# First norm of a one-layer trunk: conditioning by column blocks between the tiles of x, seven first units built tile by tile

## The chip, the cores and the metric

The kernel runs on one core of one Trainium2 chip. The number that counts is device time in microseconds (us) of one execution, as the median of several. The engines are named as the profile names them: PE multiplies matrices (PEld is its weight load), DVE, ACT and POOL work element by element, SP issues the transfers.

## The reference

One inference step of a trunk with one layer: 1024 latent tokens and 128 context tokens of width 1024 go through a SwiGLU block, a token mixer (attention and a gated recurrence) and a second SwiGLU block, each on a normalised and conditioned input. What matters here is the input of the first SwiGLU block:

```python
mod_p = (silu(c_ctx) @ w_ada[l] + b_ada[l]).reshape(1, N_MOD, D_MODEL)          # context
mod_s = (silu(c) @ w_ada[l] + b_ada[l]).reshape(c.shape[0], N_MOD, D_MODEL)     # latent
x = x + 0.5 * m[2] * swiglu(modulate(x, norm_g[0], m[0], m[1]), *ffn1)
def modulate(x, g, shift, scale): return rmsnorm(x, g) * (1.0 + scale) + shift
def swiglu(h, w1, w3, w2): return (silu(h @ w1) * (h @ w3)) @ w2
```

Shift is `m[0]`, scale is `m[1]`: 1024 numbers each for latent and for context, made from two vectors and 1024x2048 weights. The hidden width is 2816, that is 22 blocks of 128.

## The kernel before

**Layout.** Features lie on the partitions. `x` is eight tiles `x0`..`x7` of 128 features by 1152 tokens (latent first, then context). The tokens are cut into four quarters of 288 (`QW`), taken in the order `QS` = 3, 0, 1, 2; quarter 3 holds both kinds of tokens. A product in full precision is three matmuls on operands split into a high and a low part (`mm3`: high weight by high x, high weight by low x, low weight by high x).

**The first norm is folded.** The first block's units multiply the weights by `x * gs`, where `gs` is gain times (1 + scale). `split` makes the high part `bh` on ACT and the low part `bl` on DVE for one quarter of one tile (quarter 3 in two pieces of 160 and 128 tokens). The factor of each token, `rs`, is multiplied in when a unit is read out of PSUM, and the shift comes in as a bias, which is the shift vector through the same weights. A unit `(j, q)` is one of the two weight matrices (`j` = 0 for w1, 1 for w3) by one quarter: eight tiles of three matmuls, 24 in all, into one PSUM bank.

**`start`** is what comes first. It runs in four steps. First, all eight tiles are squared on ACT and summed on DVE (`stat_first`), and `stat_three` sums over partitions on PE (`nps`) and forms `rs` by Ln, Exp and a correction of three DVE operations. Second, `ada_pe(1, ...)` multiplies both vectors by the 1024x1024 scale weights: eight transfers of 512 KB (`wada`), each followed by four PE matmuls into four groups of 32 partitions; ACT copies the sums (`adar`), PE turns them (`adat`), DVE adds the bias (`modt`) and forms all of `gs`. Third, the first weights w1 and w3 were split in between (`hl`), and eight tiles are split and multiplied into six units (`up` and `dn` hold three banks each; `st` and `ps1` one each); `ada_pe(0, ...)`, the same for shift, is advanced between the tiles. Fourth, the shift is written as two extra columns beside quarter 3 (`shift`), and 16 small matmuls `pb` form the bias of the first block.

**After it**, `plain_block` runs four hidden blocks (`f` = 0 to 3) in this way, with the other two units of block 0 first; `after()` advances, between the units, `whole`, which forms the normalised input `hx` and writes it to memory (`hd`), and from block 2 on `sums`, which reads it back and forms the combined operands of the later blocks. The other 18 hidden blocks use those (`fast_block`).

**What sets the order.** Each engine runs its instructions in one order, and waits at an instruction until its operands are there; a scheduler fixes that order when the program is built. Instructions recorded under `pin` (`keep_in_program_order`) keep the order of the code on their engine. All transfers are issued by SP.

Of the kernel before, what the change touches and what calls it, by code (L numbers as in the profile page):

```python
# [9 lines left out]
F32 = mybir.dt.float32  # L10
# [83 lines left out]
class Trunk:  # L94
# [27 lines left out]
    def start(self):  # L122
        nc, a, pp = self.nc, self.a, self.pp
        self.sc = self.fp.tile([P, KT, 32], F32, name="sc")
        nc.vector.memset(self.sc, 0.0)
        nc.scalar.activation(self.sc[:, :, 0:2], self.cc, AF.Silu)
        pin = self.tc.keep_in_program_order
        wada = lambda k: self.wide("wada")
        raw = [self.wide("raw0")[:, :D].rearrange("p (k m) -> p k m", k=KT) for _ in range(2)]
        self.x = [self.tt(F32, f"x{k}") for k in range(KT)]  # L130
        self.new_rs()
        for k in range(KT):
            nc.sync.dma_start(self.x[k][:, :T], a["xT"][k])
            if k in (2, 4):
                nc.sync.dma_start(raw[k // 2 - 1], a["w13"][0, 0, k // 2 - 1])
        for k in range(KT):
            for c in ORDER:
                self.stat_first(c, k, pin)
        self.stat_three(pin)
        ws = [self.hl(raw[j], [P, KT, P], nc.vector, pin) for j in range(2)]  # L140
        for _ in self.ada_pe(1, wada, pin):
            pass
        self.alloc_b(0)
        units = [(0, q) for q in QS] + [(1, q) for q in QS[:2]]
        ps = {u: self.bank(("up", "dn")[i // 3], "ps") for i, u in enumerate(units)}
        m0 = self.ada_pe(0, wada, pin)
        for k in range(KT):
            for q in QS:
                self.split(q, k, pin)
            if k == KT - 1:  # L150
                w1 = self.load_w(a["w13"][0, 1, 0], KT, P, pin)
            for j, q in units:
                (wh, wl), (xh, xl) = ws[j], self.B[q][k // 4]
                term = wh[:, k], wl[:, k], xh[:, k % 4, :QW], xl[:, k % 4, :QW]
                self.mm3(ps[j, q], [term], start=k == 0, stop=k == KT - 1)
            for _ in range((0, 0, 0, 1, 2, 2, 2, 1)[k]):
                next(m0)
        next(m0, None)
        self.pre = ws, (w1, self.load_w(a["w13"][0, 1, 1], KT, P, pin))
        self.shift()  # L160
        self.early, self.bias = ps, []
        for j in range(2):
            pb = pp.tile([P, 2], F32, tag="ps1", bufs=1, name="pb")
            for k in range(KT):
                nc.tensor.matmul(pb, raw[j][:, k], self.modt[:, 0, k], start=k == 0, stop=k == KT - 1)
            bias = self.cp.tile([P, 2], F32, tag="bias", bufs=6, name="bias")
            nc.vector.tensor_copy(bias, pb)
            self.bias.append(bias)
# [86 lines left out]
    def ada_pe(self, m, buf, pin=lambda i: i):  # L255
        nc, a = self.nc, self.a
        ps = self.pp.tile([P, 256], F32, tag="ps1", bufs=1, name="adap")
        for k in range(KT):
            w = buf(k)[:, :D]
            pin(nc.sync.dma_start(w, a["w_ada"][k * P : (k + 1) * P, m * D : (m + 1) * D]))  # L260
            for g in range(4):
                pin(
                    nc.tensor.matmul(
                        ps[32 * g : 32 * g + 32, :],
                        self.sc[:, k, :],
# [166 lines left out]
    def stat_first(self, c, k, pin):  # L432
# [5 lines left out]
        if k:  # L438
            pin(nc.vector.tensor_add(acc, acc, sq))
# [1846 lines left out]
```

## Time and profile before

| | |
|---|---|
| runs | 2874.91, 2879.49, 2879.66 us; median 2879.49 |
| span of the profiled execution | 2874.3 us |
| busy share of the span | PE 97%, PEld 92%, DVE 70%, ACT 46%, POOL 34% |
| transfers | 331.76 MB, mean 115 GB/s |
| PE before its first matmul | 20.17 us |
| first matmul of hidden block 0 | 34.48 us |
| first matmul of hidden block 1 | 74.31 us |

The page gives no time of the profiled execution beside its span; what lies around the span is taken as the difference to the median, 5.2 us. Times of rows count from the start of the span. In a row of the timeline the columns are the start, the length, the engine, the line of the code, the operation, what it writes and reads with its shape, and how many instructions the row holds; a bracket gives idle time ahead of it and what ended that. In a row of groups the columns behind the count are the busy time, the mean length in ns, and the idle time ahead. In a row of windows they are the stretch, its length, the busy time of PE, PEld, DVE, ACT and POOL with their counts, the granted clock of PE (1.00 is full), the share of transfer engines in use and GB/s.

### The profile page before, as it was taken

Reading aid. Unit: us, or ns where it says so; the run is one execution under the profiler, and the core shown is the slowest. Engines: PE = TensorE matmul, PEld = TensorE weight load, DVE = VectorE, ACT = ScalarE, POOL = GpSimd, SP = SyncE. Lnnn points to the kernel's source line nnn. Section 1 sums busy time; section 2 is a strip of 40 time slices with the busy share of each in tenths; the row PEclk is TensorE's granted clock in tenths of the full one; section 3 lists DMA queues with packets and bytes.
Section 4 is the critical chain, followed back from the end, with each engine's and each line's share of the span. In section 5 each row is a group of like instructions: output and inputs, shape, how many; then the busy total and the mean of one; then the engine's idle time right before and its main releaser. Section 6 shows DMA issues by size and latency. Waiting matters only on the chain. (4 is left out here: it accounts for less than half of the span.)

```text
span 2874.3 us, 55665 instructions
## 1 busy us (share of the span) xinstructions
PE 2778.7 (97%) x21138; PEld 2641.1 (92%) x21138; DVE 2025.9 (70%) x4425; ACT 1331.1 (46%) x2738; POOL 966.0 (34%) x1005
## 2 busy tenths in 40 slices
PE   6999999999999999999999999989999999999998
PEld 5999999999989999988998787779989999999997
DVE  7677777577778877877355777756675666568875
ACT  6432322322166677767535777730552222236332
POOL 0133233354222122222144444532452443334450
PEclk9999999999999999999999999999999999999999
DMA  6643333663121111112412001262553443447631
GB/s 237 211 142 128 125 125 117 216 209 116 61 84 55 50 57 37 57 44 71 165 60 79 18 14 31 71 221 82 177 173 100 154 146 122 138 139 213 205 100 67
DMA packets 218940, 331.76 MB, mean 115 GB/s; under 512 B 24048, under 2 KB 142768, under 8 KB 218672
## 3 DMA queue, kind: packets, MB, share of 16 engines
q1 hardware_dynamic: 218672, 328.20, 35.0%
q8 instruction: 167, 2.74, 0.4%
q14 instruction: 101, 0.83, 0.1%
HBM read 244.93 MB, written 83.18 MB: 114 GB/s over the span
## 5 line engine op out<-in xcount | busy, mean ns | idle before, releaser
L1746 PE MATMUL b<-xo,wo 128*128 128x288 f32 x3552 | 482.3, 295 | 0.3 <-DVE et L1752 0.3
L1746 PEld LDWEIGHTS b<-xo,wo 128*128 128x128 f32 x3552 | 474.3, 188 | 0.6 <-DVE et L1752 0.6
L1746 PE MATMUL b<-bh,wo 128*128 128x288 f32 x1776 | 365.0, 295 | 2.1 <-ACT et L1756 2.1
L473 PE MATMUL mm<-xh,wh 128*128 128x384 f32 (+1 forms) x1008 | 352.1, 349 | 10.9 <-DVE sg L750 5.6
L474 PE MATMUL mm<-xl,wh 128*128 128x384 f32 (+1 forms) x1008 | 341.9, 339 | 0.0
L475 PE MATMUL mm<-xh,wl 128*128 128x384 f32 (+1 forms) x1008 | 341.3, 339 | 0.0
L1746 PEld LDWEIGHTS b<-bh,wo 128*128 128x128 f32 x1776 | 288.6, 188 | 2.3 <-ACT et L1756 2.3
L502 DVE SCALAR_TENSOR_TENSOR x<-dn,modt,x 128x256 f32<-128x256 f32 (+4 forms) x472 | 225.6, 499 | 89.5 <-PE dn L475 88.4
L1746 PE MATMUL b<-bl,wo 128*128 128x288 f32 x888 | 261.4, 294 | 0.0
L473 PEld LDWEIGHTS mm<-xh,wh 128*128 128x128 f32 (+1 forms) x1008 | 189.4, 188 | 20.8 <-DVE sg L750 7.4
L1720 ACT CAST wo<-raw 128x512 fp32r<-128x512 f32 x185 | 114.7, 621 | 183.9 <-issue 78.9
L474 PEld LDWEIGHTS mm<-xl,wh 128*128 128x128 f32 (+1 forms) x1008 | 189.4, 188 | 2.3 <-issue 0.7
L475 PEld LDWEIGHTS mm<-xh,wl 128*128 128x128 f32 (+1 forms) x1008 | 189.1, 188 | 1.0
L1946 PE MATMUL d<-xd,wd 128*128 128x288 f32 x1344 | 181.4, 297 | 6.6 <-DVE x L1933 5.9
L1946 PEld LDWEIGHTS d<-xd,wd 128*128 128x128 f32 x1344 | 179.9, 190 | 8.0 <-DVE x L1933 2.8
L318 DVE SCALAR_TENSOR_TENSOR junk<-wada,cb 128x512 bf16<-128x512 f32 x224 | 164.4, 734 | 14.1 <-DMA wada<-in_w_aT 13.3
L1721 DVE TENSOR_TENSOR wo<-raw,wo 128x512 fp32r<-128x512 f32 x185 | 127.4, 689 | 65.3 <-ACT wo L1720 62.6
L1461 POOL TENSOR_TENSOR ehl<-e,ehl 128x512 fp32r<-128x512 f32 x93 | 122.1, 1317 | 141.6 <-ACT ehl L1459 76.2
L1746 PEld LDWEIGHTS b<-bl,wo 128*128 128x128 f32 x888 | 167.1, 188 | 0.0
L247 POOL TENSOR_TENSOR wl<-raw,wh 128x1024 fp32r<-128x1024 f32 (+3 forms) x51 | 101.2, 1985 | 171.1 <-ACT wh L246 154.8
L1720 ACT CAST wo<-ws 128x512 fp32r<-128x512 f32 x74 | 45.6, 618 | 225.9 <-POOL ws L1716 216.9
L1721 DVE TENSOR_TENSOR wo<-ws,wo 128x512 fp32r<-128x512 f32 x74 | 71.6, 968 | 109.3 <-ACT wo L1720 109.0
(441 smaller groups left out, 7193.4 us busy)
## 6 DMA issues: line engine op xcount, KB each, us to landing
raw<-in_w SPq DMA_DIRECT2D x148, 256.0 KB, 3.5
wada<-in_w_aT SPq DMA_DIRECT2D x112, 256.0 KB, 3.1
raw<-in_w SPq DMA_DIRECT2D x42, 512.0 KB, 3.8
raw<-in_w_in SPq DMA_DIRECT2D x41, 512.0 KB, 3.5
xr<-xd SPq DMA_DIRECT2D x56, 288.0 KB, 3.7
hr<-hs SPq DMA_DIRECT2D x26, 576.0 KB, 5.7
hb<-hd SPq DMA_DIRECT2D x44, 288.0 KB, 3.4
hs<-et SPq DMA_DIRECT2D x84, 144.0 KB, 2.1
```

Source lines behind the costliest of these rows:

```text
L247: pin((eng or self.nc.gpsimd).tensor_sub(wl, raw, wh))
L318: nc.vector.scalar_tensor_tensor(junk, ws[n % 2], 1.0, cs[s], ALU.mult, ALU.mult, accum_out=o)
L473: pin(nc.tensor.matmul(ps, wh, xh, start=start and i == 0, stop=False))
L474: pin(nc.tensor.matmul(ps, wh, xl, start=False, stop=False))
L475: pin(nc.tensor.matmul(ps, wl, xh, start=False, stop=stop and i == n - 1))
L502: nc.vector.scalar_tensor_tensor(self.x[m][:, a:b], ps[:, a - lo : b - lo], self.modt[:, gm, m, s : s + 1], self.x[m][:, a:b], ALU.mult, A ...
L1461: eng.tensor_sub(el, e, eh)
L1720: nc.scalar.copy(wh, src[i])
L1721: nc.vector.tensor_sub(wl, src[i], wh)
L1746: nc.tensor.matmul(ps, w[:, k], x[:, k, :QW], start=first, stop=last, skip_group_check=home != i)
L1946: nc.tensor.matmul(ps, w[:, k], xv, start=start, stop=stop, skip_group_check=home != i)
```

## The change

The conditioning weights for scale and shift are laid out by blocks of 128 output columns (`w_a01`), one block for each tile of `x`. The transfers now go tile by tile: w1, tile 0, its two blocks of conditioning weights (512 KB each), w3, tile 1, its two blocks, and so on, all pinned. For each tile, `sums` multiplies both vectors by the two blocks in 16 PE matmuls, ACT copies the result, and `vectors` turns it by one matmul with a selector that also adds the two halves; four small DVE operations make `gs` and the shift of that tile, and the shift's high and low part as two extra columns of quarter 3. `split` of tile k then runs quarter by quarter, each followed by its units; seven of the eight units of block 0 grow tile by tile. The `sums` of tile k + 1 stand behind the units of quarter 3 of tile k, its `vectors` behind those of quarter 0. The squares of tile k + 1 (two halves of 576 tokens) follow the splits of tile k on ACT and are added on POOL, those of the last tile on DVE. Behind the last tile `stat` and `root` form `rs` in three chunks between the quarters, the eighth unit (w3 by quarter 2) runs as a whole, and `pb` is gone: the two extra columns of the units (0, 3) and (1, 3) are the bias. `whole` is advanced in block 1 only.

The new `start`, and the other places, cut to their core (the old `start`, `ada_pe`, `shift`, `stat_first` and `stat_three` are removed):

```diff
     def start(self):
+        nc, a, pp, fp = self.nc, self.a, self.pp, self.fp
         pin = self.tc.keep_in_program_order
+        sc = fp.tile([P, KT, 32], F32, name="sc")
+        nc.vector.memset(sc, 0.0)
+        nc.scalar.activation(sc[:, :, 0:2], self.cc, AF.Silu)
+        sel = fp.tile([P, 2, 2], F32, name="sel")
+        iv = self.ident.rearrange("p (v h r) -> p v h r", v=2, h=2)
+        nc.vector.tensor_add(sel, iv[:, :, 0, 0:2], iv[:, :, 1, 0:2])
+        b1 = fp.tile([P, KT], F32, name="b1")
+        nc.vector.tensor_scalar(b1, self.bada[:, 1], 1.0, None, ALU.add)
+        raw = [self.wp.tile([P, KT, P], F32, tag="raw", bufs=2, name="raw") for _ in range(2)]
         self.x = [self.tt(F32, f"x{k}") for k in range(KT)]
         self.new_rs()
+        self.alloc_b(0)
+        wa = {}
+
+        def load(what):
+            for c in what:
+                if c in "ab":
+                    j = "ab".index(c)
+                    pin(nc.sync.dma_start(raw[j], a["w13"][0, 0, j]))
+                elif c == "w":
+                    k = len(wa)
+                    wa[k] = [self.wide("wada")[:, :D].rearrange("p (k n) -> p k n", k=KT) for _ in range(2)]
+                    for v in range(2):
+                        pin(nc.sync.dma_start(wa[k][v], a["w_a01"][k, v]))
+                else:
+                    k = int(c)
+                    pin(nc.sync.dma_start(self.x[k][:, :T], a["xT"][k]))
+
+        def sums(k):
+            ps = pp.tile([P, P], F32, tag="ps1", bufs=1, name="adap")
+            for i in range(4):
+                for g in range(4):
+                    n = 4 * (g % 2) + i
+                    pin(
+                        nc.tensor.matmul(
+                            ps[32 * g : 32 * g + 32, :],
+                            sc[:, n, :],
+                            wa[k][g // 2][:, n, :],
+                            start=(i == 0),
+                            stop=(i == 3),
+                            tile_position=(0, 32 * g),
+                            skip_group_check=True,
+                        )
+                    )
+            row = fp.tile([P, P], F32, tag="hf", bufs=self.hfb, name="adar")
+            pin(nc.scalar.copy(row, ps))
+            return row
+
+        def vectors(k, row):
+            ps = pp.tile([P, 2, 2], F32, tag="ps1", bufs=1, name="adat")
+            pin(nc.tensor.matmul(ps, row, sel, start=True, stop=True))
+            ng = self.ng[:, 0, k : k + 1].to_broadcast([P, 2])
+            pin(nc.vector.scalar_tensor_tensor(self.gs[:, 0, k], ps[:, 1], b1[:, k : k + 1], ng, ALU.add, ALU.mult))
+            sh = self.modt[:, 0, k]
+            pin(nc.vector.tensor_scalar(sh, ps[:, 0], self.bada[:, 0, k : k + 1], None, ALU.add))
+            hi, lo = [t[:, k % 4, QW : QW + 2] for t in self.B[QS[0]][k // 4]]
+            pin(nc.vector.tensor_copy(hi, sh))
+            pin(nc.vector.tensor_sub(lo, sh, hi))
+
+        def square(k):
+            for v in range(2):
+                c = ts(v, 2 * QW)
+                sq = self.rs[:, c] if k == 0 else self.half("sq")
+                pin(nc.scalar.activation(sq, self.x[k][:, c], AF.Square))
+                if k:
+                    pin((nc.vector if k == KT - 1 else nc.gpsimd).tensor_add(self.rs[:, c], self.rs[:, c], sq))
+
+        load("a0wb1w")
+        ws = [self.hl(raw[j], [P, KT, P], nc.vector, pin) for j in range(2)]
+        square(0)
+        vectors(0, sums(0))
+        rest = iter(("2w", "3w", "4w", "5w", "6w", "7w", "", ""))
+        homes = {(0, 3): "up", (1, 3): "dn", (0, 0): "up", (1, 0): "dn", (0, 1): "up", (1, 1): "dn", (0, 2): "st"}
+        cols = {q: QW + 2 * (q == QS[0]) for q in QS}
+        ps = {u: self.bank(t, "ps", cols[u[1]]) for u, t in homes.items()}
+
+        def unit(j, q, k):
+            (wh, wl), (xh, xl), n = ws[j], self.B[q][k // 4], cols[q]
+            term = wh[:, k], wl[:, k], xh[:, k % 4, :n], xl[:, k % 4, :n]
+            self.mm3(ps[j, q], [term], start=k == 0, stop=k == KT - 1, pin=pin)
+
+        var = []
+
+        def stat(c):
+            p = pp.tile([P, CW], F32, tag="ps1", bufs=1, name="nps")
+            cs = slice(c * CW, (c + 1) * CW)
+            pin(nc.tensor.matmul(p, self.ones, self.rs[:, cs], start=True, stop=True))
+            v = self.half("var")[:, :CW]
+            pin(nc.scalar.copy(v, p))
+            var.append((self.rs[:, cs], v))
+
+        def root():
+            r, v = var.pop(0)
+            t = fp.tile([P, CW], F32, tag="hf", bufs=self.hfb, name="rt")
+            pin(nc.scalar.activation(r, v, AF.Ln, bias=self.epst))
+            pin(nc.scalar.activation(r, r, AF.Exp, scale=-0.5))
+            pin(nc.vector.scalar_tensor_tensor(t, v, EPS, r, ALU.add, ALU.mult))
+            pin(nc.vector.scalar_tensor_tensor(t, t, -0.5, r, ALU.mult, ALU.mult))
+            pin(nc.vector.scalar_tensor_tensor(r, t, 1.5, r, ALU.add, ALU.mult))
+
         for k in range(KT):
+            load(next(rest))
+            last = k == KT - 1
+            if last:
+                self.lnexp()
+            for i, q in enumerate(QS):
+                self.split(q, k, pin)
+                unit(0, q, k)
+                if q != QS[-1]:
+                    unit(1, q, k)
+                if last:
+                    if i:
+                        root()
+                    if i < 3:
+                        stat(ORDER[i])
+                elif i == 0:
+                    row = sums(k + 1)
+                elif i == 1:
+                    vectors(k + 1, row)
+            if not last:
+                square(k + 1)
+        w1 = self.load_w(a["w13"][0, 1, 0], KT, P, pin)
+        ps[1, QS[-1]] = self.bank("ps1", "ps")
         for k in range(KT):
+            unit(1, QS[-1], k)
         self.pre = ws, (w1, self.load_w(a["w13"][0, 1, 1], KT, P, pin))
+        self.early = ps
...
         early = not l and not f
         for j, q in order:
             wh, wl = ws[j]
-            if early and (j, q) in self.early:
+            n = QW + (2 if not l and q == QS[0] else 0)
+            if early:
                 ps = self.early[j, q]
             else:
-                n = QW + (2 if not l and f and q == QS[0] else 0)
                 ps = self.bank("up", "ps", n)
...
-            if early:
-                bias[j] = self.bias[j]
+            if n > QW:
+                bias[j] = self.cp.tile([P, 2], F32, tag="bias", bufs=6, name="bias")
+                nc.vector.tensor_copy(bias[j], ps[:, QW:n])
...
                 if l and f == 0:
                     next(self.tail, None)
-                elif f < 2 - l:
+                elif f == 1 - l:
                     next(steps, None)
-                else:
+                elif f:
                     next(sums, None)
...
-    a["w_ada"] = f("w_ada")[0]
+    a["w_a01"] = f("w_ada")[0][:, : 2 * D].reshape(KT, P, 2, KT, P).transpose(3, 2, 1, 0, 4)
```

The order on PE at the start before: all three sums over partitions (`nps`), then all 32 matmuls of the scale (`adap`), two turns (`adat`), and only then the first unit (`ps`, with `bh`, `bl` the split of x and `wh`, `wl` that of the weight).

```order
L446 MATMUL nps<-rs,ones 128x384 x3
L263 MATMUL adap<-wada,sc 32x256 x32
L278 MATMUL adat<-ident,adar 128x128 x2
L473 MATMUL ps<-bh,wh 128x288
L474 MATMUL ps<-bl,wh 128x288
L475 MATMUL ps<-bh,wl 128x288
```

The order on PE now, in the middle of tile 1 (the end of the sums for tile 2, `adap_271`; the two units of quarter 0, `ps_184` and `ps_185`; the turn for tile 2, `adat_298`; the first unit of quarter 1, `ps_186`):

```order
L159 MATMUL adap_271<-wada_190,sc_100 32x128 x2
L159 MATMUL adap_271<-wada_191,sc_100 32x128 x2
L497 MATMUL ps_184<-bh_118,wh_147 128x288
L498 MATMUL ps_184<-bl_119,wh_147 128x288
L499 MATMUL ps_184<-bh_118,wl_148 128x288
L497 MATMUL ps_185<-bh_118,wh_151 128x288
L498 MATMUL ps_185<-bl_119,wh_151 128x288
L499 MATMUL ps_185<-bh_118,wl_152 128x288
L175 MATMUL adat_298<-sel_103,adar_288 128x4
L497 MATMUL ps_186<-bh_122,wh_147 128x288
```

The conditioning of the next tile now stands inside the units of each tile.

DVE before, from the one `gs` of all tiles on: nothing stands between the low parts of one tile and those of the next.

```order
L334 SCALAR_TENSOR_TENSOR gs_93<-modt_92,vec_68 128x16
L467 SCALAR_TENSOR_TENSOR bl_292<-x0_105,gs_93,bh_291 128x160
L467 SCALAR_TENSOR_TENSOR bl_292<-x0_105,gs_93,bh_291 128x128
L467 SCALAR_TENSOR_TENSOR bl_280<-x0_105,gs_93,bh_279 128x288
L467 SCALAR_TENSOR_TENSOR bl_284<-x0_105,gs_93,bh_283 128x288
L467 SCALAR_TENSOR_TENSOR bl_288<-x0_105,gs_93,bh_287 128x288
L467 SCALAR_TENSOR_TENSOR bl_292<-x1_106,gs_93,bh_291 128x160
```

DVE now, in tile 0 (`bl_119`, `bl_123`, `bl_127` are the low parts of quarters 0, 1 and 2; `gs_93`, `modt_92` and the two small ones behind them belong to tile 1):

```order
L491 SCALAR_TENSOR_TENSOR bl_119<-x0_109,gs_93,bh_118 128x288
L177 SCALAR_TENSOR_TENSOR gs_93<-adat_231,b1_105,vec_68 128x2
L179 TENSOR_SCALAR modt_92<-adat_231,vec_68 128x2
L181 CAST bh_130<-modt_92 128x2
L182 TENSOR_TENSOR bl_131<-modt_92,bh_130 128x2
L491 SCALAR_TENSOR_TENSOR bl_123<-x0_109,gs_93,bh_122 128x288
L491 SCALAR_TENSOR_TENSOR bl_127<-x0_109,gs_93,bh_126 128x288
L491 SCALAR_TENSOR_TENSOR bl_131<-x1_110,gs_93,bh_130 128x160
```

The low part of quarter 1 now stands behind the four small operations for the next tile.

POOL now, from its first work on; before, the six `wl` (L247) came first and nothing stood ahead of them.

```order
L2297 UNCONDITIONAL_BRANCH
L190 ISA
L190 TENSOR_TENSOR rs<-rs,sq 128x576 x12
L330 TENSOR_TENSOR wl<-raw,wh 128x1024 x6
L1740 TENSOR_TENSOR ws<-raw 128x256 x2
```

Twelve additions of squares moved from DVE to POOL.

DVE now, at the last tile (`rt` and `rs` are the root of one chunk, `sl` a unit's read-out):

```order
L491 SCALAR_TENSOR_TENSOR bl_121<-x7_116,gs_93,bh_120 128x288
L221 SCALAR_TENSOR_TENSOR rt_676<-var_666,rs_117 128x384
L222 SCALAR_TENSOR_TENSOR rt_676<-rt_676,rs_117 128x384
L223 SCALAR_TENSOR_TENSOR rs_117<-rt_676,rs_117 128x384
L1692 TENSOR_TENSOR sl_755<-ps_182,rs_117 128x288
L491 SCALAR_TENSOR_TENSOR bl_125<-x7_116,gs_93,bh_124 128x288
L221 SCALAR_TENSOR_TENSOR rt_694<-var_684,rs_117 128x384
L222 SCALAR_TENSOR_TENSOR rt_694<-rt_694,rs_117 128x384
L223 SCALAR_TENSOR_TENSOR rs_117<-rt_694,rs_117 128x384
L1692 TENSOR_TENSOR sl_759<-ps_184,rs_117 128x288
L491 SCALAR_TENSOR_TENSOR bl_129<-x7_116,gs_93,bh_128 128x288
```

The low parts of the last two quarters stand behind the roots of the first two chunks.

100 lines of the change are left out of this document (3 added, 97 removed).

## The prediction

> **What bounds the kernel now.** I read the page first, then PE by stretches, then PE's order of time up to hidden block 1, then the prices of single operations.
>
> ```profile
> span 2874.3 us, 55665 instructions
> PE 2778.7 (97%) x21138; PEld 2641.1 (92%) x21138; DVE 2025.9 (70%) x4425; ACT 1331.1 (46%) x2738; POOL 966.0 (34%) x1005
> ...
> 20.00:40.00 20.00, 14.94 (x101) 9.16 (x102) 14.00 (x32) 13.49 (x28) 0.00 (x0) 0.83 0.84 325
> 60.00:74.30 14.30, 14.03 (x90) 13.44 (x83) 11.14 (x33) 13.24 (x19) 2.36 (x1) 0.76 0.34 106
> 74.40:99.60 25.20, 25.20 (x192) 25.20 (x191) 10.74 (x30) 10.67 (x21) 4.79 (x2) 1.00 0.82 272
> 99.60:124.90 25.30, 25.30 (x192) 25.30 (x192) 24.80 (x59) 12.47 (x29) 5.06 (x2) 1.00 0.63 200
> 124.90:150.10 25.20, 25.20 (x192) 25.20 (x191) 15.64 (x32) 10.05 (x20) 4.66 (x5) 1.00 0.50 148
> ```
>
> PE is the bound, and from hidden block 1 on it has no gap: 25.20 of 25.20 us for 192 matmuls. So whatever moves the start of block 1 moves the end by as much, and the change is judged by that one moment.
>
> ```profile
> PE nps L446 <- DVE rs L439: 20.2, 1, 20.2
> 31.08 1.01 PE L263 MATMUL adap<-wada,sc 128*32 128x256 f32 x8 [1.63 <-DMA wada<-in_w_ada]
> 34.48 0.61 PE L473 MATMUL ps<-bh,wh 128*128 128x288 f32 x1 [1.23 <-ACT bh L466]
> 62.17 1.95 PE L165 MATMUL pb<-modt,raw 128*128 128x2 f32 x16 [0.27 <-DVE modt L279]
> 65.39 3.48 PE L165 MATMUL pb<-modt,raw 128*128 128x2 f32 x16
> 74.31 0.29 PE L473 MATMUL ps<-bh,wh 128*128 128x290 f32 x1
> ```
>
> PE waits 20.2 us for the squares and then for the scale weights; units run from 34.48 with no wait worth naming, `pb` takes 5.4 us, and block 1 starts at 74.31. The change works on these 74.31 us.
>
> **Its parts, and the sum.** Removed: `pb` (5.4 us of PE, and 0.76 of the clock around it), the wait for all squares and all scale weights. The eight units of block 0 stay: 192 matmuls. The transfers are the same bytes in another order; their pace:
>
> ```profile
> GB/s 0 76 238 326 412 426 418 424 408 430 399 412 414 410 407 407 393 139 382 404 418 421 410 407 262 11 0 0 0 0 0 52 246 393 311 333 74 79 270 0
> 11.99 2.78 ACT L437 ACTIVATE sq<-x 128x384 f32<-128x384 f32 x6 [1.37 <-DMA x<-in_xT]
> ```
>
> Slices are 1.5 us: 1.58 MB are in at 7.5 us, then 0.41 MB each us. The fourth tile (3.0 MB in that order) is there by this count at 11.0, and ACT got it at 11.99: 1 us from bytes to use. Now w1, tile 0, two blocks and w3 are 2.8 MB with the constants: 10.5 + 1.1 = 11.6 us. ACT splits w3 only then (1.0), squares tile 0 (two of 576: 1.25) and copies the sums; with the turn and `gs` (1.2) the first split starts at 15.1; its two pieces (0.8) and six matmuls at half clock (1.5) bring PE to the sums of tile 1 at 17.4. A tile and its blocks are 1.64 MB, 4.0 us. If transfers set the pace, tile 7 would be there near 40 us.
>
> They don't, as the order shows: a tile is one chain across PE, ACT and DVE. Its prices:
>
> ```profile
> 49.02 1.07 PE L263 MATMUL adap<-wada,sc 128*32 128x256 f32 x16
> 50.02 0.40 PE L473 MATMUL ps<-bh,wh 128*128 128x288 f32 x1
> ...
> 50.39 0.30 PE L475 MATMUL ps<-bh,wl 128*128 128x288 f32 x1
> 50.52 0.30 PE L473 MATMUL ps<-bh,wh 128*128 128x288 f32 x1
> 60.49 0.37 ACT L275 COPY adar<-adap 128x256 f32<-128x256 f32 x1 [7.39 <-PE adap L263]
> 60.99 0.38 PE L278 MATMUL adat<-ident,adar 128*128 128x128 f32 x2
> L466 ACT ACTIVATE bh<-x,gs 128x288 fp32r<-128x288 f32 x24 | 11.0, 525 | 0.0
> L467 DVE SCALAR_TENSOR_TENSOR bl<-x,gs,bh 128x288 fp32r<-128x288 f32 x24 | 11.0, 514 | 0.1
> 33.50 0.17 DVE L334 SCALAR_TENSOR_TENSOR gs<-modt,vec 128x16 f32<-128x16 f32 x1
> ```
>
> From the sums of tile k + 1 to those of tile k + 2: 16 matmuls over the same columns as the eight at 49.02, 1.00; copy 0.37; high part of quarter 0, 0.52; its low part, 0.51; the five matmuls that wait for it, 0.135 each, 0.67; the turn, between half of 0.38 and all of it, 0.25; `gs`, shift and its two parts, three lengths of 0.17, 0.5; low part of quarter 1, 0.51; then 5 + 3 + 6 matmuls, 1.89; six hand-overs, 0.5 (the first matmul after a switch lasts 0.40 against 0.30; as much is taken for the others). Sum 6.7 us, and nothing of it overlaps, since each engine keeps its order. ACT's other work (two more quarters, two squares) fits beside it.
>
> The additions on POOL are the next term. Before, POOL had nothing to do here. What it does to DVE is seen later:
>
> ```profile
> 98.74 0.45 DVE L1633 TENSOR_TENSOR xo<-hd,xo 128x288 fp32r<-128x288 f32 x1
> 101.07 2.46 POOL L247 TENSOR_TENSOR wl<-raw,wh 128x1024 fp32r<-128x1024 f32 x1 [10.36 <-ACT wh L246]
> 101.19 2.65 DVE L1633 TENSOR_TENSOR xo<-hd,xo 128x288 fp32r<-128x288 f32 x1
> 145.44 1.95 POOL L1716 TENSOR_TENSOR ws<-raw 128x256 f32<-128x256 f32 x2 [27.00 <-DVE bl L1594]
> 146.72 0.98 DVE L1683 SCALAR_TENSOR_TENSOR sl<-hf,bias,sl 128x288 f32<-128x288 f32 x1
> 151.97 0.51 DVE L1683 SCALAR_TENSOR_TENSOR sl<-hf,bias,sl 128x288 f32<-128x288 f32 x1
> L2089 POOL TENSOR_TENSOR hl<-hr,hh 128x576 fp32r<-128x576 f32 x4 | 6.0, 1516 | 1.9 <-PE d L1946 1.9
> ```
>
> A DVE operation of 0.45 that starts behind a POOL operation lasts 2.65 us, to just behind POOL's end; one of the form of `bl`, with two operands in SBUF, goes from 0.51 to 0.98. So DVE stands still for the length of the POOL operation. An addition of 576 is 1.38 in proportion to 1024 in 2.46, and 1.52 in the row of 576 with its waits; I take 1.42. There are two for each of tiles 1 to 6. The first is ready when half the tile is squared, on ACT 2.3 us behind the sums (copy 0.37, three quarters at 11.0 / 24, half a square 0.6); `gs` comes 2.6 us behind them (0.37 + 0.52 + 0.51 + 0.67 + 0.25 and hand-overs). So they take the port first: the cast of the shift waits for the first, its low part for the second, and the low part of quarter 1 starts at 6.2 instead of 4.2. I take +2.1 a tile, cycle 8.8 (ends: 0, and 2 x 1.52 = 3.0).
>
> That leaves PE all but idle for about 3.1 us in each tile. What gaps do to its clock:
>
> ```profile
> 168.00:171.00 3.00, 2.04 (x16) 1.81 (x14) 0.58 (x1) 0.62 (x1) 3.00 (x5) 1.00 0.05 19
> 171.00:174.00 3.00, 1.84 (x13) 1.85 (x14) 2.96 (x8) 2.26 (x5) 0.10 (x1) 1.00 0.09 18
> ...
> 1527.40:1529.40 2.00, 0.00 (x0) 0.00 (x0) 0.35 (x1) 0.28 (x1) 1.92 (x4) 1.00 0.69 250
> 1529.50:1532.50 3.00, 2.85 (x10) 2.85 (x11) 1.31 (x3) 1.62 (x5) 1.16 (x3) 0.53 0.49 195
> ```
>
> About 2.1 us of idle across 171 left 1.00; 2.0 and a little more ahead of 1529.4 brought 0.53 for 3 us. With 3.1 I take a fall in each tile, 3.2 us at 0.53, which loses 0.47 of them: +1.5, cycle 10.3 (ends: 0, and the whole cycle at half clock). The Trainium skill, page "TensorE: Matmul & The Clock Gate", section "The HAM clock gate", has the clock fall only after an idle window of about 3.4 us; by that rule a gap of 3.1 may pass, the cycle would stay 8.8 and block 1 start at 90.5. The trace does not bear it out in full: 2.0 us was enough at 1527, though not at 170.
>
> Behind the sums of tile 7 the rest of `start` is again one chain:
>
> ```profile
> L356 ACT ACT_TABLE_LOAD x1 | 1.3, 1283 | 0.0
> L365 ACT ACTIVATE rs<-nps,epst 128x384 f32<-128x384 f32 x3 | 1.7, 581 | 0.5 <-PE nps L446 0.2
> L367 DVE SCALAR_TENSOR_TENSOR rt<-nps,rs 128x384 f32<-128x384 f32 x3 | 1.7, 554 | 2.3 <-ACT rs L366 2.3
> L446 PE MATMUL nps<-rs,ones 128*128 128x384 f32 x6 | 4.2, 874 | 20.2 <-DVE rs L439 20.2
> ...
> 72.89 1.35 DVE L1574 TENSOR_TENSOR hx<-x,rs 128x1152 f32<-128x1152 f32 x1
> ```
>
> Sums, copy, three quarters, two squares and the table on ACT, 5.2; tile 7's quarter 3 with the last additions, 2.9; one `nps`, 0.64 at full clock (4.2 for three at half); copy, quarter 0, Ln and Exp, 2.3; three `rt` and a read-out, 2.2, then the low part of quarter 1, 0.5; the same for the next chunk, 2.7, with 0.4 of hand-overs; two matmuls 0.3, and the eighth unit 3.2: 20.4, and 1.5 for one more spell of low clock. POOL's `wl` for block 1 ends about then too.
>
> Sum: 17.4 + 6 x 10.3 + 20.4 + 1.5 = 101.1 us for the start of block 1, against 74.31: +26.8. Costed at nothing: `whole`, now all in block 1, beside PE. DVE has 10.74 of 25.20 us filled there; eight `hx` of 1.35 and block 0's read-outs (some 6) bring it to about 25 with the first `sums` pushed back, and block 3 has 9.6 us free to catch up. Without that cover a read-out would be late by one `hx`, 1 to 3 us once. The columns 289 and 290 cost 48 matmuls under 0.1 us. The profiled execution (2874.3) would become 2901; I put the same 26.8 on the median 2879.49, which is 5.2 above it: 2906.
>
> **Rivals.** *Lock without clock* (0.20): the gap of 3.1 us passes, cycle 8.8: 17 + 53 + 20.4 = 90.5, +16, 2896. For it: the rows at 168. *No lock* (0.12): the additions fall where DVE reads nothing else, cycle 6.7: 78, +3.5, 2883. Against it: they are ready 0.3 us ahead of `gs`, in each tile. *Low clock throughout* (0.11): PE is never busy long enough to rise; its 3.8 us in the cycle grow by 3.0, cycle 11.9: +38, 2918. *Faster* (0.07): the chain closes up and the transfers set the pace, 4.0 a tile: 17 + 24 + 20.4 = 61.5, -13, 2867. It decides below a cycle of 5.2, where block 1 starts 5.7 us earlier than before. For it: PE, ACT and DVE are each busy under 4.5 us a tile, and 20 us of idle PE are there to be won; against it: the order allows no overlap of two tiles.
>
> **Numbers.** The likeliest (0.50) is 2906, its own range 2897 to 2915. Eight in ten: 2883 to 2919 leaves out *Faster*, half of *No lock* and the top of *Low clock*. About 0.2%, 5.8 us, is what can be told from no change here: faster 0.07, same 0.12 (*No lock*), slower 0.81.
>
> **What would show it.** Right: the first unit on PE near 16 us, sums (L159) at a spacing of 9 to 11 us, `bl` of quarter 1 at over 1.5 us in length beside L190 on POOL, a clock under 0.9 between 20 and 90 us, block 1 near 100 us, and from there the same length as before. Wrong: sums at 4 to 6 us, `bl` at 0.51 beside POOL, or a gap in PE behind block 1's start, which would mean that DVE's work there has no cover.

## The result, and the profile after

The changed kernel takes 2913.03 us (median of four runs, 2909.41 to 2919.38), the kernel before 2877.2 beside it (four runs): a ratio of 1.0126, interval 1.0114 to 1.0138, 35.8 us slower. 2906 was forecast. The profiled execution is the run of 2919.38, the longest of the four; the rows are read for where time lies, the medians for how much. In the experiments below, one of six executions of e5_nopb took 5399.04 us, far from the others, and is left out of its median.

From the page of the changed kernel:

```profile
span 2917.6 us, 55903 instructions
PE 2801.7 (96%) x21246; PEld 2659.0 (91%) x21246; DVE 2037.5 (70%) x4421; ACT 1332.7 (46%) x2739; POOL 982.9 (34%) x1017
```

Four stretches, each from the sums of one tile to those of the next, and the tail behind the last sums (columns as above: PE, PEld, DVE, ACT, POOL, clock, transfers):

```profile
28.80:39.00 10.20, 6.25 (x56) 5.32 (x55) 4.52 (x9) 3.36 (x8) 2.76 (x2) 0.85 0.72 282
49.40:59.70 10.30, 6.33 (x57) 5.35 (x56) 4.51 (x9) 3.36 (x8) 2.75 (x2) 0.83 0.00 0
59.70:70.00 10.30, 6.33 (x56) 5.36 (x56) 4.51 (x9) 3.38 (x8) 2.76 (x2) 0.83 0.00 0
70.00:80.30 10.30, 6.34 (x56) 5.40 (x55) 4.51 (x9) 3.36 (x8) 2.76 (x2) 0.83 0.01 2
80.30:105.80 25.50, 19.50 (x101) 14.28 (x101) 14.45 (x30) 14.83 (x27) 3.49 (x2) 0.67 0.00 1
```

No engine is full in a tile of 10.3 us, and from 49.40 on the transfers are done: the tile is a chain of waits. PE's order of time shows it, from the turn of one tile to the sums of the next, then the last sums and block 1's first matmul:

```profile
42.45 0.28 PE L175 MATMUL adat<-sel,adar 128*128 128x4 f32 x2
42.58 0.38 PE L497 MATMUL ps<-bh,wh 128*128 128x288 f32 x1
45.89 0.46 PE L498 MATMUL ps<-bl,wh 128*128 128x288 f32 x1 [2.93 <-DVE bl L491]
46.15 0.44 PE L499 MATMUL ps<-bh,wl 128*128 128x288 f32 x1
...
49.04 0.45 PE L499 MATMUL ps<-bh,wl 128*128 128x290 f32 x1
49.41 1.10 PE L159 MATMUL adap<-wada,sc 128*32 128x128 f32 x32
...
80.31 1.08 PE L159 MATMUL adap<-wada,sc 128*32 128x128 f32 x32
...
105.86 0.30 PE L497 MATMUL ps<-bh,wh 128*128 128x290 f32 x1
```

PE waits 2.93 us for the low part of quarter 1; the matmuls behind it are 0.24 us apart instead of 0.13: half clock, until the next sums. Why DVE is late stands in its own and POOL's order of time, in tile 2 first and then in tile 6, where the additions (those of tile 7's squares) are DVE's own:

```profile
42.64 2.75 POOL L190 TENSOR_TENSOR rs<-rs,sq 128x576 f32<-128x576 f32 x2 [7.55 <-ACT sq L188]
42.76 0.22 DVE L177 SCALAR_TENSOR_TENSOR gs<-adat,b,vec 128x2 f32<-128x2 f32 x1 [1.14 <-PE adat L175]
43.14 0.92 DVE L181 CAST bh<-modt 128x2 fp32r<-128x2 f32 x1
44.10 1.31 DVE L182 TENSOR_TENSOR bl<-modt,bh 128x2 fp32r<-128x2 f32 x1
45.33 0.93 DVE L491 SCALAR_TENSOR_TENSOR bl<-x,gs,bh 128x288 fp32r<-128x288 f32 x2
...
83.91 0.22 DVE L177 SCALAR_TENSOR_TENSOR gs<-adat,b,vec 128x2 f32<-128x2 f32 x1 [1.14 <-PE adat L175]
84.29 0.17 DVE L181 CAST bh<-modt 128x2 fp32r<-128x2 f32 x1
84.49 0.16 DVE L182 TENSOR_TENSOR bl<-modt,bh 128x2 fp32r<-128x2 f32 x1
```

Two operations on 256 numbers last 0.92 and 1.31 us beside POOL's additions and 0.17 and 0.16 without them. The first addition ends near 44.0 and the second near 45.4, and so do they; `gs`, which reads PSUM, keeps its 0.22. Below, this standing still of DVE beside POOL is called the lock.

Where the 35.8 us are: block 1 starts at 105.86 instead of 74.31, +31.6. From there to the fast blocks (first `b` from `bh`) it takes 81.8 instead of 76.5, +5.2. The first `b`, before and after:

```profile
L1746 PE MATMUL b<-bh,wo x1776: 288/295/373, 150.8 to 2594.2; 128*128 128x288 f32 x198
```

```profile
L1770 PE MATMUL b<-bh,wo x1776: 288/295/370, 187.6 to 2633.9; 128*128 128x288 f32 x198
```

PE's waits between block 1's start and the fast blocks:

```profile
PE ps L497 <- DVE hf L1703: 1.9, 1, 1.9
PE ps L497 <- DVE sl L1692: 0.8, 1, 0.8
```

The window around the longer one, at 157:

```profile
156.00:162.00 6.00, 4.74 (x25) 4.77 (x26) 6.00 (x18) 2.56 (x7) 0.00 (x0) 0.73 0.73 230
```

2.7 us of waiting, and a clock of 0.73 in the window: from 158.7 to 162.0 PE runs at half clock (0.51), which loses another 1.6. The other 0.9 of the 5.2 has no row of its own. Before, PE had no wait there. The sum to the fast blocks is 36.8 us, near the 35.8 of the medians. The profiled executions differ by 43.3; of the 6.5 us more, 2.9 lie between the first and the last `b` and 3.6 behind it; the medians do not show them, and they were not followed up.

### The profile page after: what moved, and what is told of

Read it like the earlier page. It is cut to its first block, busy times and chain, and to the rows that moved or that the text cites. A ratio compares the mean times of both kernels' runs of the same rounds, so it can differ in the third digit from the quotient of the medians.

```text
span 2917.6 us, 55903 instructions
## 1 busy us (share of the span) xinstructions
PE 2801.7 (96%) x21246; PEld 2659.0 (91%) x21246; DVE 2037.5 (70%) x4421; ACT 1332.7 (46%) x2739; POOL 982.9 (34%) x1017
## 5 line engine op out<-in xcount | busy, mean ns | idle before, releaser
L1744 ACT CAST wo<-raw 128x512 fp32r<-128x512 f32 x185 | 114.7, 621 | 197.4 <-PE b L1770 83.4
L1485 POOL TENSOR_TENSOR ehl<-e,ehl 128x512 fp32r<-128x512 f32 x93 | 122.1, 1318 | 141.0 <-ACT ehl L1483 80.9
L498 PE MATMUL ps<-bl,wh 128*128 128x288 f32 (+1 forms) x448 | 142.8, 319 | 21.6 <-DVE bl L491 19.3
L497 PE MATMUL ps<-bh,wh 128*128 128x288 f32 (+1 forms) x448 | 142.0, 318 | 17.4 <-ACT bh L490 10.4
```

The lines of the kernel that those rows point to most:

```text
L497: pin(nc.tensor.matmul(ps, wh, xh, start=start and i == 0, stop=False))
L498: pin(nc.tensor.matmul(ps, wh, xl, start=False, stop=False))
L1485: eng.tensor_sub(el, e, eh)
L1744: nc.scalar.copy(wh, src[i])
```

## Experiments

All numbers at once (the kernel before ran beside each group, with medians of 2876.6 to 2878.5 in the later ones); the cycle is the distance of the sums of two tiles late in the series, the tail runs from the last sums to block 1's start, and the column behind it from there to the first `b`.

| kernel | cycle | tail | block 1 | to `b` | median | ratio to before |
|---|---|---|---|---|---|---|
| before | | | 74.31 | 76.5 | 2877.2 | |
| after | 10.3 | 25.55 | 105.86 | 81.8 | 2913.03 | 1.0114 to 1.0138 |
| e3_fill | 8.84 | 20.38 | 91.78 | 78.1 | 2898.41 | 1.0053 to 1.0087 |
| e2_noadd | 6.89 | 20.33 | 83.42 | 80.5 | 2891.81 | 1.0039 to 1.0069 |
| e1_dve | 8.0 to 9.4 | 20.32 | 92.25 | 79.3 | 2900.17 | 1.0067 to 1.0097 |
| e6_fill8 | 10.4 | 20.58 | 100.87 | 82.8 | 2910.64 | 1.0100 to 1.0131 |
| e4_tail | 10.3 | 17.30 | 97.88 | 80.7 | 2907.97 | 1.0089 to 1.0119 |
| e7_wdve | 10.3 | 26.04 | 107.78 | 76.0 | 2911.54 | 1.0109 to 1.0137 |
| e5_nopb | | | 66.38 | 79.1 | 2868.11 | 0.9956 to 0.9981 |
| p1_twotiles | 4.65 | 16.05 | 58.30 | 79.9 | 2864.77 | 0.9947 to 0.9977 |
| e8_p1pool | 4.85 to 5.00 | 16.24 | 61.23 | 80.9 | 2869.47 | 0.9956 to 0.9981 |
| p2_weights | 4.65 | 16.05 | 59.17 | 76.7 | 2861.40 | 0.9929 to 0.9969 |
| p3_turn | 4.22 | 15.00 | 57.29 | 76.3 | 2861.46 | 0.9931 to 0.9958 |

**The clock alone (e3_fill).** Work of no effect fills PE's gap; lock and chain stay.

```diff
                 elif i == 1:
                     vectors(k + 1, row)
+                    for _ in range(16):
+                        n = cols[QS[0]]
+                        pin(nc.tensor.matmul(ps[0, QS[0]], zw, self.B[QS[0]][k // 4][0][:, k % 4, :n], start=False, stop=False))
```

> Edit: additions stay on POOL; 16 matmuls with a weight of zeros (290 columns, 0.133 us apart, 2.1 us) are put on PE behind the turn of each tile, in the 2.93 us for which PE waits for the low part of quarter 1. They add nothing to the sums. Theory (the clock falls because of that gap): the clock stays at 1.00 in the tiles, the 14 matmuls behind the gap are 0.135 apart instead of 0.24, spacing 10.3 becomes 8.8, block 1 starts 7 x 1.5 = 10 us earlier (95 to 97), time 2902 to 2905. Rival (the clock falls for the low use of PE over a longer stretch, or the chain hides it): spacing 10.3 or more, 2913; if the fillers run at half clock they take 3.9 us, 1 us more than the gap, and spacing is 11.3, block 1 at 112, 2920.

Windows of that run, one tile and the tail:

```profile
53.70:62.60 8.90, 7.06 (x76) 6.15 (x76) 4.56 (x9) 3.37 (x8) 2.81 (x2) 1.00 0.01 2
71.40:91.80 20.40, 15.61 (x118) 12.41 (x118) 13.09 (x29) 13.71 (x25) 2.19 (x1) 1.00 0.00 1
```

Full clock in the tiles and in the tail. The cycle is 8.84, so the clock had cost 1.47 us a tile, as expected. The tail is 20.38 instead of 25.55, which the expectation did not count: block 1 starts 3 us ahead of the 95 to 97 given, and the time is under its range. Doing more work made the kernel 14.6 us faster.

**The lock alone (e2_noadd).** No additions for tiles 1 to 6.

```diff
-                if k:
-                    pin((nc.vector if k == KT - 1 else nc.gpsimd).tensor_add(self.rs[:, c], self.rs[:, c], sq))
+                if k == KT - 1:
+                    pin(nc.vector.tensor_add(self.rs[:, c], self.rs[:, c], sq))
```

> Edit: the additions of tiles 1 to 6 are left out, so the first norm is formed from the squares of tiles 0 and 7 alone. This is the chain without any price of the additions. Theory: 6.7 us a tile (the sum of the prediction without its terms for POOL and for the clock), block 1 at 105.86 - 6 x 3.6 - 1 = 83, time 2890; the gap of PE is then under 1 us and the clock holds in the tiles. Rival (the chain was under-counted and POOL's part is small): spacing 9 to 10.3, block 1 at 98 to 105, 2905 to 2913. The difference to the run with the additions on DVE is what 1.4 us of DVE cost on the chain of a tile: 1.3 to 1.8 us by the theory, 0 if DVE has room.

```profile
42.40:49.30 6.90, 4.84 (x56) 3.98 (x55) 2.62 (x9) 3.38 (x8) 0.00 (x0) 1.00 0.19 75
56.20:63.10 6.90, 4.84 (x59) 3.97 (x58) 2.61 (x9) 3.37 (x8) 0.00 (x0) 1.00 0.01 4
```

The bare chain is 6.89. Against the 8.84 of the run before, both at full clock, the lock costs 1.95 us a tile. The first two cycles took 9.1 us, at half clock for most of them, which is why block 1 starts at 83.4 and not at 78. That this is the 83 expected is luck: the expectation left the tail near its 25.55, and it came out at 20.33, at full clock, while the first two cycles took 4.8 us more than the 6.7 each.

**Additions on DVE (e1_dve).**

```diff
-                    pin((nc.vector if k == KT - 1 else nc.gpsimd).tensor_add(self.rs[:, c], self.rs[:, c], sq))
+                    pin(nc.vector.tensor_add(self.rs[:, c], self.rs[:, c], sq))
```

> Edit: all additions of squares on DVE, none on POOL. Theory (POOL's additions hold DVE for their length and the gap that follows lets PE's clock fall): the tiles take what tile 7 takes in the trace of the changed kernel, whose additions are on DVE already: from its sums at 80.31 to the end of the next two units at 88.84, 8.5 us, or 8.0 where the clock holds. Six tiles of 10.3 become 8.0 to 8.5, the cast and the low part of the shift go from 0.92 and 1.0 to 0.17 us each, block 1 starts at 92 to 95 instead of 105.86, time 2899 to 2903. Rival 1 (the chain of hand-overs alone is 10.3, POOL's lock costs nothing): spacing 10.3, 2913, or slower by the 1.4 us of DVE per tile (up to 11.7, block 1 at 114, 2921). Rival 2 (lock is the whole of it and DVE's additions are hidden): spacing 6.7, block 1 at 84, 2891.

```profile
27.70:35.70 8.00, 5.11 (x56) 4.00 (x55) 3.95 (x11) 3.37 (x8) 0.00 (x0) 1.00 1.00 400
53.10:62.50 9.40, 7.33 (x56) 6.04 (x55) 3.95 (x11) 3.37 (x8) 0.00 (x0) 0.68 0.00 0
71.90:92.20 20.30, 13.80 (x101) 10.31 (x101) 13.01 (x29) 13.64 (x24) 2.11 (x1) 1.00 0.00 1
```

At full clock the cycle is 8.0: 1.1 us above the bare chain for 1.42 us of additions. But only the second of the six cycles was that short: the next two took 8.7 (clock 0.80 and 0.89), the last two 9.4 (0.68 and 0.69), and the first 10.0, its matmuls 0.24 us apart. No wait of PE in these later tiles is longer than 1.03 us, three to a tile. So a fall of the clock does not need one long gap. Block 1's start and the time came out in the forecast ranges, but by luck: the cycles were longer than 8.0 to 8.5, and the tail, at full clock, was 5.2 us shorter than the one the forecast kept.

**Half the fillers (e6_fill8).** 8 instead of 16.

> Edit to the changed kernel: 8 matmuls with a weight of zeros behind the turn of each tile instead of the 16 of the earlier run. PE's longest gap falls from 2.93 to 1.85 us; with 16 it was 0.87 and the clock stayed at 1.00. Theory of a single gap (the clock falls after one idle stretch of 2 to 3 us): it stays at 1.00, spacing 8.84, block 1 at 92, 2898, as with 16. Theory of the share (the clock falls when PE's busy share over several us is low; the run with the additions on DVE fell to half clock with no gap over 1.03 us): it falls in some or all tiles, spacing 9.3 to 10.3, block 1 at 97 to 105, 2903 to 2912.

```profile
59.50:69.90 10.40, 7.49 (x65) 6.43 (x64) 4.54 (x9) 3.37 (x8) 2.78 (x2) 0.83 0.01 2
```

```profile
66.63 0.40 PE L503 MATMUL ps<-bl,wh 128*128 128x288 f32 x1 [1.87 <-DVE bl L496]
```

The gap is 1.87 us and the clock falls in every tile, to the same 0.83 as with 2.93; the cycle does not move. The tail happened to run at full clock here (20.58), but the way to the fast blocks was 1.0 us longer than in the changed kernel, and the runs of the two overlap (2908.88 to 2912.37 against 2909.41 to 2919.38). What sets the fall is not settled: two gaps of 0.87 and 1.03 us in each tile of 6.9 (no additions) and two of 0.87 in each of 8.84 (16 fillers) let it stand, three of 0.87 to 1.03 in tiles of 8.0 (additions on DVE) did not for long.

The tail does not settle it either. PE waits 1.06 us behind its first statistic in the changed kernel, at half clock, and with the 16 fillers, at full clock:

```profile
87.00:104.00 17.00, 13.37 (x37) 9.13 (x38) 9.21 (x20) 8.50 (x15) 1.69 (x1) 0.50 0.00 0
91.38 0.61 PE L497 MATMUL ps<-bh,wh 128*128 128x288 f32 x1 [1.06 <-ACT bh L490]
```

```profile
81.19 0.40 PE L502 MATMUL ps<-bh,wh 128*128 128x288 f32 x1 [1.06 <-ACT bh L495]
```

The same three waits, of 1.00 to 1.06 us, stand in the tails of e1_dve, e2_noadd and e6_fill8, and all four tails took 20.3 to 20.6 us at full clock. So these waits alone do not bring the clock down.

**The tail's order (e4_tail).** The four splits of the last tile stand ahead of its statistics.

```diff
             if last:
                 self.lnexp()
+                for q in QS:
+                    self.split(q, k, pin)
             for i, q in enumerate(QS):
-                self.split(q, k, pin)
+                if not last:
+                    self.split(q, k, pin)
```

> Edit to the changed kernel: in the last tile all four splits stand ahead of the three statistics; nothing else. In the trace of the changed kernel each of the last three splits stands on ACT behind the copy of a statistic, which waits for PE, and PE then waits 1.06 us for that split, three times. Theory (the tail is long because its steps wait for each other in turn, and at half clock): PE has no wait between 88.84 and the last unit; three statistics (4.4 us at half clock) and five units (3.6) end near 97 instead of 102.2, block 1 starts at 100 to 101, time 2907 to 2909. Rival (only the clock is to blame): the tail stays at 25 us, 2913. Second rival: the clock rises as PE has no more gaps, and the tail falls to 18 to 20, block 1 at 99, 2906.

```profile
85.00:90.00 5.00, 3.72 (x17) 3.13 (x17) 4.31 (x12) 2.90 (x6) 0.00 (x0) 0.77 0.00 0
90.00:95.00 5.00, 4.74 (x24) 3.62 (x23) 2.42 (x5) 4.04 (x8) 0.00 (x0) 0.89 0.00 0
```

The tail is 17.30 us; PE's three waits of 1.06 us are gone, and the clock, which had fallen, rises in it (0.89 at 90 to 95, then 1.00), so it is the second rival, and more than it gave. Of 8.0 us at block 1's start the medians show 5.1.

**Block 1's weights (e7_wdve).** Requested in tile 5, low parts on DVE.

```diff
+            if k == 5:
+                raw1 = self.wp.tile([P, KT, P], F32, tag="raw", bufs=2, name="raw")
+                pin(nc.sync.dma_start(raw1, a["w13"][0, 1, 0]))
...
             if last:
                 self.lnexp()
+                w1 = self.hl(raw1, [P, KT, P], nc.vector, pin)
...
-        self.pre = ws, (w1, self.load_w(a["w13"][0, 1, 1], KT, P, pin))
+        self.pre = ws, (w1, self.hl(raw2, [P, KT, P], nc.vector, pin))
```

> Edit to the changed kernel: only the two weight blocks of hidden block 1 are moved, as in the run with two tiles and early weights: requested in tile 5, low parts on DVE (1.23 us each), the first inside the last tile. It is to price what PE waits for behind the start of block 1 (81.7 us from there to the fast blocks against 76.5 before). Theory (POOL's 5.3 us at 102.3 hold DVE, its queue of read-outs, hx and sums then runs late, and PE waits 0.8 and 1.9 us for it in blocks 2 and 3, with a spell of low clock): block 1 starts at 105 to 106 as before the edit, or up to 1 us later, the fast blocks 77 us behind it, time 2908 to 2910. Rival (the eight hx in block 1 alone are the cause): 81 to 82 us stay, 2913.

The way from block 1 to the fast blocks is 76.0 us, 5.8 shorter, with all eight `hx` still in block 1 and one wait of 0.9 us left. So the `hx` alone do not make the waits; they went when POOL's weight splits were taken out of the way. In the changed kernel these stand at the very end of the tail:

```profile
102.31 5.33 POOL L330 TENSOR_TENSOR wl<-raw,wh 128x1024 fp32r<-128x1024 f32 x2 [26.09 <-DVE hf L1703]
103.01 2.37 DVE L223 SCALAR_TENSOR_TENSOR rs<-rt,rs 128x384 f32<-128x384 f32 x1
109.29 3.10 DVE L1707 SCALAR_TENSOR_TENSOR sl<-hf,bias,sl 128x288 f32<-128x288 f32 x2
```

The splits do not set the size of the waits by themselves: e3_fill, e1_dve and e2_noadd keep them and the eight `hx`, and PE waits 0.5, 1.6 and 2.5 us there (78.1 to 80.5 to the fast blocks). The start of block 1 is 1.9 us later (1.4 of them ahead of the last sums), more than the 1 expected, and the median, 2911.54, is above the 2908 to 2910 expected and gains only 1.5 us, inside its spread. That the splits take part in the wait is shown, a gain of the time is not.

**What `pb` had cost (e5_nopb).** In the kernel before, `pb` is left out.

```diff
-            pb = pp.tile([P, 2], F32, tag="ps1", bufs=1, name="pb")
-            for k in range(KT):
-                nc.tensor.matmul(pb, raw[j][:, k], self.modt[:, 0, k], start=k == 0, stop=k == KT - 1)
             bias = self.cp.tile([P, 2], F32, tag="bias", bufs=6, name="bias")
-            nc.vector.tensor_copy(bias, pb)
+            nc.vector.memset(bias, 0.0)
```

> Edit to the kernel before: the product pb of the shift and the first two blocks of weights (32 matmuls of two columns) is left out and the bias of hidden block 0 set to zero, so the shift is missing in block 0. It prices what the change removes there. Theory: 5.4 us of PE and a clock of 0.76 around them lie on the path, block 1 starts at 68 to 69 instead of 74.31, time 2870.5 to 2871.5 against 2876.6. Rival (the read-outs of block 0 hold block 1's first bank anyway): block 1 at 72 to 74, 2875 to 2877.

Block 1 starts 7.9 us earlier (0.7 of them ahead of where `pb` stood), the fast blocks 5.4, and the median of its five other runs is 10.4 us less (by the interval 5.5 to 12.7). The share of the change that removes `pb` is a gain, above the forecast at block 1's start and equal to it at the fast blocks. The difference lies behind block 1's start, where PE now waits for DVE, though nothing else of the change is in this kernel:

```profile
PE ps L470 <- DVE hf L1676: 1.3, 1, 1.3
PE ps L470 <- DVE sl L1667: 0.5, 2, 0.4
```

**Two tiles under way (p1_twotiles).** The chain is cut at the tile boundary.

```diff
-        load("a0wb1w")
+        load("a0wbw1w2w")
...
+                if i == 0 and not last:
+                    r = row(psums[k + 1])
                 unit(0, q, k)
...
                 elif i == 0:
-                    row = sums(k + 1)
+                    t = turn(r)
                 elif i == 1:
-                    vectors(k + 1, row)
+                    vec(k + 1, t)
+                    if k + 2 < KT:
+                        psums[k + 2] = sums(k + 2)
```

> Edit: one tile further ahead. The sums of tile k + 2 stand in tile k behind the units of quarter 0 (they read blocks of weights that are requested one tile earlier than x), the copy of the row stands behind the first split of tile k + 1, and the turn, gs and the shift of tile k + 1 in tile k. All additions on DVE; in the last tile the four splits stand ahead of the three statistics. Theory (what bounds the tiles is one chain over PE, ACT and DVE, which no longer spans a tile boundary): PE is the bound with 24 x 0.133 + 1.1 = 4.3 us a tile or the transfers with 4.0; first unit at 15 to 16, tile 7 at 46 to 50, tail 10 to 14, block 1 at 58 to 62 against 74.31 before, time 2865 to 2870, faster than before by 9 to 14. Rival (hand-overs between the engines cost as much as before wherever they stand): spacing 7 to 8.5, block 1 at 85 to 95, 2890 to 2902.

```profile
28.30:32.90 4.60, 4.43 (x56) 3.87 (x55) 3.81 (x12) 3.37 (x9) 0.00 (x0) 1.00 1.02 409
37.60:42.20 4.60, 4.43 (x56) 3.89 (x55) 3.81 (x12) 3.38 (x9) 0.00 (x0) 1.00 0.73 289
```

The same work per tile, with the additions on DVE, takes 4.65 us instead of 10.3 (8.0 at best in the old order). PE is now near full (4.43 of 4.60 us), DVE busy for 3.8 of them, the transfers full until they run out, and the kernel is faster than before. Block 1 and the time (0.2 us below its range) came out at the early end of what was given, though the cycle was 0.35 us longer than 4.3 and the tail 2 us longer than 14.

**The lock in the new order (e8_p1pool).** As the last run, with the additions of tiles 1 to 6 on POOL.

> Edit to the first run with two tiles under way: the additions of tiles 1 to 6 are on POOL again, in the order of work of that run. Theory (the lock prices DVE, not the order): DVE has 3.85 us of work a tile, of which 1.42 are additions; on POOL these become 2 x 1.4 us in which DVE operations with two operands in SBUF stand still, so DVE needs 2.4 + up to 2.8 = 5.2 us a tile, spacing 4.65 becomes 4.9 to 5.4, block 1 at 60 to 64 instead of 58.3, time 2867 to 2871 against 2864.8. Rival (with two tiles under way there is slack and the lock is hidden): spacing 4.4 to 4.65, 2862 to 2865. Second rival (gaps bring the clock down as well): spacing 7 or more, block 1 above 75, 2882.

DVE of that run, in tile 3 (`gs` and the shift of tile 4):

```profile
34.36 0.22 DVE L186 SCALAR_TENSOR_TENSOR gs<-adat,b,vec 128x2 f32<-128x2 f32 x1 [0.92 <-PE adat L178]
34.75 0.34 DVE L190 CAST bh<-modt 128x2 fp32r<-128x2 f32 x1
35.12 1.33 DVE L191 TENSOR_TENSOR bl<-modt,bh 128x2 fp32r<-128x2 f32 x1
```

The lock is still there (0.34 and 1.33 us for the two small operations), but the cycle is only 0.2 to 0.35 us longer than with the additions on DVE; in the old order that difference was 0.84 at full clock (8.84 against 8.0). With another tile to work on, PE's longest wait in a tile is 0.37 to 0.51 us. The clock stays at 1.00, and cycle, block 1 and median are as expected. The profiled execution, 2861.60 us, is the shortest of five, the others take 2869 to 2871, so these rows are not read for the time.

**The best versions (p2_weights, p3_turn).** Two tiles, with block 1's weights as above:

> Edit to the run with two tiles under way: block 1's two weight blocks are requested in tile 5, their low parts are formed on DVE (1.23 us each by the trace) instead of POOL (2.5 us each, which hold DVE), the first of them inside the last tile. Theory: PE's wait of 0.90 us for that low part goes, two DVE operations of 2.53 and 2.38 us fall back to 0.56, block 1 starts at 57 to 58 and the fast blocks 78 us behind it instead of 79.9; 2861 to 2863 against 2864.8. Rival (the 1.23 us on DVE delay the statistics' roots by as much): block 1 at 59, 2864 to 2866.

PE's wait for POOL is gone and the way to the fast blocks falls by 3.2 us. The last sums were 0.9 us later in this execution, so block 1 itself starts no earlier (59.17, expected 57 to 58). Then the turn ahead of the units of quarter 0, and tile 0's row ahead of its squares:

```diff
-        square(0)
-        vectors(0, row(sums(0)))
+        r0 = row(sums(0))
+        square(0)
+        vectors(0, r0)
...
-                    r = row(psums[k + 1])
+                    t = turn(row(psums[k + 1]))
...
-                elif i == 0:
-                    t = turn(r)
```

> Edit to the run with two tiles and early weights: the turn of tile k + 1 stands ahead of the units of quarter 0 of tile k instead of behind them, and the row of tile 0 is copied before its squares. Theory: DVE no longer waits 0.72 us a tile for the turn, and PE no longer 0.17 for the low part of quarter 0; spacing 4.65 becomes PE's own 4.4 to 4.5, first unit 1 us earlier, block 1 at 55.5 to 57 instead of 59.2, time 2857 to 2860 against 2861.4 and 2878 before. Rival (PE or the transfers are the bound, the waits of DVE cost nothing): 4.65, block 1 at 58, 2860 to 2862.

```profile
29.60:33.80 4.20, 4.20 (x56) 3.85 (x55) 3.93 (x13) 3.32 (x10) 0.00 (x0) 1.00 1.02 408
```

PE is full in the tiles (4.20 of 4.20), a cycle of 4.22; the first unit came only 0.2 us earlier (16.81) and not 1, since it now stands behind the turn of tile 1. Block 1 and the fast blocks start 1.9 and 2.2 us earlier than in the run before it, but the medians, 2861.46 and 2861.40, do not tell the two apart, and the 2857 to 2860 expected were not reached. Both are 16 to 17 us faster than the kernel before that ran beside them, and some 50 faster than the changed one.

## Why the prediction was right, and where it was short

The sign and the mechanism held: block 1's start was the moment to judge by, and the tiles are one chain across three engines.

- *Sums of tile 1 at 17.4*: 17.64.
- *Cycle 10.3 = 6.7 + 2.1 + 1.5*: 10.26 to 10.35 from the second cycle on, and each term was measured apart: 6.89 for the chain, 1.95 for the lock, 1.47 for the clock. The first cycle took 11.16, its matmuls 0.24 us apart from end to end; those 0.9 us were not foreseen.
- *Gaps of 3.1 us bring the clock down*: the gap was 2.93 and the clock 0.83 to 0.85 in each tile from the second on. The Trainium skill, page "TensorE: Matmul & The Clock Gate", section "The HAM clock gate", has an idle window of about 3.4 us for a fall, and by it the cycle would have been 8.8; the measured 10.3 goes against a reading of that as one gap.
- *Tail of 20.4 + 1.5*: this term was mis-sized. The chain was right (20.3 to 20.6 in four runs at full clock), the clock was not: PE ran at half clock from 87 to 104 us, which cost 5.2 us instead of 1.5. The prediction charged one spell of 3.2 us. Once down, the clock did not rise while PE met a wait of 1.06 us behind each statistic, and without these waits it did (e4_tail); but the same waits stand in the four runs at full clock, so why it fell in this tail is open.
- *Everything behind block 1's start at nothing*: this failed. It named the price without cover (1 to 3 us once, a read-out behind an `hx`) and a gap in PE there as a sign of being wrong, which came. It did not name POOL's weight splits at 102.3, without which the waits are 0.9 instead of 2.7 us; and the longer wait was followed by a fall of the clock that cost another 1.6 of the 5.2.
- *`pb` at 5.4, with 0.76 of clock around it*: 7.9 at block 1's start, 5.4 at the fast blocks.
- *`bl` of quarter 1 at over 1.5 us beside POOL*, a sign of being right, did not come, and by the prediction's own sum it could not: the cast and the shift's low part take the wait (0.92 and 1.31), and this `bl` starts behind POOL's additions, at 6.3 us from the sums (6.2 forecast), and lasts 0.5.

Block 1's start was forecast 26.8 us later and came 31.6 later; the 4.8 more are 3.7 from the tail, 0.9 from the first cycle, 0.2 from the start. With 5.2 behind it, this is the way from 26.8 to 36.8; the medians differ by 35.8.

Of the rivals, *Lock without clock* gave 8.8, 90.5 and 2896; the fillers made it true, at 8.84, 91.78 and 2898. *No lock* gave 6.7; without the additions it was 6.89. For two thirds of the tail *Low clock throughout* came true; its own 11.9 a cycle gives 109 for block 1, and the 112 behind its +38 needs 3 us more that it does not name. *Faster* was said to be barred by the order, which allows no overlap of two tiles, and the run that allows it reached 58.3 for block 1 against the 61.5 given there.

## What to carry to other kernels

Where a step goes engine to engine and back, its price is the sum of its parts, however little each engine is busy: put the head of the next step's chain one step earlier, and the engines fill. Price the clock with the gaps: the gap ahead of PE in each tile was paid for in waiting (2.93 us) and again in clock (1.47), and a forecast must ask at each stage, the last one too, whether PE is busy enough for the clock to come back. And look for what POOL does while DVE is on the path: an addition that is moved off DVE was cheaper on DVE.

## What the runs showed of the hardware

The clock fell in tiles whose longest wait was 1.03 us, and with 1.87 it fell as with 2.93; 16 more matmuls without effect kept it at 1.00. The Trainium skill, page "TensorE: Matmul & The Clock Gate", section "A second HAM failure mode: psum-queue depth-cycling", tells of clocks that swing because PE idles briefly but often; the tiles with additions on DVE agree with it (9.4 instead of 8.0 us at 0.68). It gives no threshold, and these runs don't either: four tails with three waits of 1.00 to 1.06 us kept full clock, and that of the changed kernel ran at 0.50 for 17 us.

POOL's lock holds even operations of two columns, 1.31 us instead of 0.16, and a cast with one operand in SBUF, 0.92 instead of 0.17; `gs`, which reads PSUM, lasts 0.22 beside POOL and without it.
